# Attention scores in two neighbouring PSUM banks read by one masked maximum, and the outputs moved into the projections' banks

## The chip, the core and the metric

The kernel runs as one program on one core of a Trainium2 chip. A core has a matrix engine (PE, TensorE), whose weight loads are listed apart as PEld, a vector engine (DVE), an activation engine (ACT), GpSimd (POOL) and a queue engine that issues DMAs (SP). Matmul results land in PSUM, which has eight banks of 512 float32 columns on 128 partitions. Each engine works through its own instructions in the order in which the built program lists them, and waits where a semaphore tells it to. The metric is the device time of one execution in microseconds; smaller is better.

## What is computed

The reference is two layers of a diffusion backbone over 512 latent tokens and 256 context tokens of width 1024. The change touches layer 0, a windowed attention with 16 query heads in 4 groups, one key and value head for each group. It is computed in blocks of 128 queries. A latent block sees its neighbours on both sides and all 256 context tokens, and each head has one learned extra logit, the sink:

```python
s_ctx = jnp.einsum('bqkgd,bnkd->bkgqn', qb, k_c) * scale
s_loc = jnp.einsum('bqkgd,bnkd->bkgqn', qb, kb) * scale
s_loc = jnp.where(valid, s_loc, NEG_INF)
p = jax.nn.softmax(jnp.concatenate([s_ctx, s_loc, sink_col], axis=-1), axis=-1)
out = einsum('bkgqn,bnkd->bqkgd', p[ctx], v_c) + einsum('bkgqn,bnkd->bqkgd', p[loc], vb)
```

Context blocks see the 256 context tokens and the sink alone. After the attention come an output projection, a gated feed-forward layer for both streams, and a second layer (a retention mixer and another feed-forward layer).

## The kernel before, in words

The whole program is written with a tile framework: the author writes operations on tiles from pools, and a scheduler fixes the order of the instructions on each engine when the program is built. It takes ready instructions by their place in the source, and a tile of a pool is given out in the order of the source, when the tile that held its buffer before is free. So the pools' buffer counts decide what can run ahead of what.

For each of the 4 groups (line 831) six blocks are attended: four latent blocks of 128 queries (b = 0 to 3) and two context blocks, in an order that differs between the groups (line 833). `attend` (line 760) handles one block:

- `score` (line 678), for each of the 4 heads of the group: matmuls of the head's queries with the keys into a bank (L703), and one DVE instruction (L704) that adds the mask, writes the masked scores to the SBUF tile `pr` and leaves their running extreme in a column of `stat`. Blocks with b = 0 and 3 have 512 keys, context blocks 256: one bank and one instruction. Blocks with b = 1 and 2 have 640 keys, 384 local and 256 of context: two banks and two instructions, the second starting from the first one's result. Every second head, the pair's exponentials (ACT, L101 by its helper), the reciprocal of their sums (DVE, L714) and the scaling (DVE L720 for one head, ACT L718 for the other) follow.
- `turn` (line 724), for each 128 keys: four transposes on PE into a bank of the pool `pT` (L729), and one copy to SBUF (L731, ACT for even pieces, DVE for odd ones).
- `output` (line 736): the products with the values (L743) into a bank `pO`, and a copy out of it (L758, or the two halves of `split` in the last group).

`make_q` (line 559) makes two heads' queries: 24 matmuls of 512 columns for the latent stream and 24 of 256 columns for the context (L147 to L149, by the helper `mm3`), each into a bank `pj`, the square sums that give the norms (L610) into a third `pj` tile, and between them the rotation and the splitting into two parts on DVE and ACT (`shape`, line 581). It is called after the blocks i = 1 and i = 3 of the groups 0 to 2 (line 835), for the next group's heads. In the last group `context_out` (line 818) projects the finished context outputs, each into a `pj` tile.

The eight banks are used thus: two `pj` (projections, line 66), two `pT` (line 283), one `pO` (line 284), three `S2` for scores (line 662). During the set-up before the attention `pO` holds the context keys (`kvc`, line 412), and three banks of a pool that is closed later hold the values (line 413). SBUF buffers that limit how far a block can run ahead: nine `pr` tiles and eight `tt` tiles.

Of the kernel before, what the change touches and what calls it, by code (L numbers as in the profile page):

```python
# [12 lines left out]
ALU = mybir.AluOpType  # L13

P = 128
# [3 lines left out]
SC = 256  # L19
# [30 lines left out]
def dit_kernel(ctx, tc, xT, cT, crow, small, consts, masks, tabs0, tabs1, jtab, adaQ, adaN, adaT, wst, out):  # L50
    nc = tc.nc
    mult, add, sub = ALU.mult, ALU.add, ALU.subtract
# [9 lines left out]
    def T(pool, cols, tag, bufs, dt=F32):  # L62
        return pool.tile([P, cols], dt, tag=tag, bufs=bufs, name=tag)

    def pj(n=512):
        return T(psJ, 512, "pj", 2)[:, :n]
# [33 lines left out]
    def lnexp(*args, **kw):  # L100
        ins = nc.scalar.activation(*args, **kw)  # L101
        after(ins, [turn["pre"]])
        turn["lnexp"].append(ins)
        return ins
# [31 lines left out]
    def next_w(pool, own=2, raw=None, behind=(), late=()):  # L136

        raw = raw or w_raw()
        w = w_parts(pool, own)
        after(split(raw, *w, behind), late)  # L140
        return w
# [21 lines left out]
    def split(t, hi, lo, behind=()):  # L163
        after(nc.scalar.copy(hi, t), behind)  # L164
        return nc.vector.tensor_tensor(lo, t, hi, op=sub)  # L165
# [66 lines left out]
    def h_tiles(s):  # L232
        hi = t_h(s)
        if s == 0:
            return hi, t_h(s)
        return hi[:, 0:SC], hi[:, SC:2 * SC]
# [44 lines left out]
    psA = A.enter_context(tc.tile_pool(name="psA", bufs=1, reuse_waits="tile", space=PSUM))  # L281
    hpool[0] = A.enter_context(tc.tile_pool(name="hA", bufs=1, reuse_waits="tile", side="right"))
    pT = lambda: T(psA, 512, "pT", 2)
    pO = lambda: T(psA, 512, "pO", 1)

    def cond_columns(pool):

# [81 lines left out]
    ps_v = psS.enter_context(tc.tile_pool(name="psS", bufs=1, reuse_waits="tile", space=PSUM))  # L369
# [31 lines left out]
    mask = T(akv, NM * P, "mask", 1, BF16)  # L401
# [7 lines left out]
    wu = [first_unit] + [unit_load(u) for u in UNITS[1:]]  # L409

    kvx = [pj(), pj()]
    kvc = pO()
    kvv = [T(ps_v, 512, "kvv", 3) for _ in range(3)]

    def busy(n):
# [108 lines left out]
    kx, kc = {}, {}  # L524
# [134 lines left out]
        vt.append(v)  # L659
    psS.close()  # L660
    psA2 = At.enter_context(tc.tile_pool(name="psA2", bufs=1, reuse_waits="tile", space=PSUM))
    pS = lambda: T(psA2, 512, "S2", 3)

    run_dep = mybir.DependencyInfo(mybir.DependencyClass.Sync, mybir.DependencyReason.DATA)
    o_raw = {}
# [2 lines left out]
    class Block:  # L668
# [9 lines left out]
        def score(self, i):  # L678
            g, s, b, n = self.g, self.s, self.b, len(self.keys) * P
            hd, nl = 4 * g + i, len(self.lk) * P  # L680
            if i % 2 == 0:
                self.st = T(ap, 16, "stat", 4)
            st, c = self.st, 2 * (b + 4 * s)
            qt = q[hd, s][:, b * P:(b + 1) * P]
            pt = T(ap, 656, "pr", PRB)[:, :n + 1]
            top = stats[hd][:, 1, c + hd % 2:c + hd % 2 + 1]
            nc.gpsimd.tensor_copy(pt[:, n:n + 1], top)
            lo, x0 = st[:, i % 2:i % 2 + 1], self.lk[0] * P if nl else 0

            if nl == 384:  # L690
                runs = [(nl, SC, 5 * P, [(0, SC, kc)]), (0, nl, 2 * P, [(0, nl, kx)])]
            elif nl == 0:
                runs = [(0, SC, 5 * P, [(0, SC, kc)])]
            elif b == 0:
                runs = [(0, n, 3 * P, [(0, nl, kx), (nl, SC, kc)])]
            else:
                runs = [(0, n, 0, [(0, SC, kc), (SC, nl, kx)])]
            for c0, w, m0, parts in runs:
                bank = pS()[:, :w]
                for p0, pw, kk in parts:  # L700
                    for r in range(2):
                        keys = kk[g][r] if kk is kc else kk[g][r][:, x0:x0 + pw]
                        nc.tensor.matmul(bank[:, p0:p0 + pw], qt, keys, start=r == 0, stop=r == 1)  # L703
                nc.vector.tensor_tensor_reduce(pt[:, c0:c0 + w], bank, mask[:, m0:m0 + w], 1.0, top, add, ALU.min, lo)  # L704
                top = lo
            self.pr.append(pt)
            if i % 2 == 0:
                return
            y = stats[hd][:, 0, c:c + 2]
            nc.vector.scalar_tensor_tensor(st[:, 2:4], st[:, 0:2], -1.0, y, mult, mult)  # L710
            for e in range(2):
                pt = self.pr[i - 1 + e]
                lnexp(pt, pt, AF.Exp, scale=y[:, e:e + 1], bias=st[:, 2 + e:3 + e], accum_out=st[:, 4 + e:5 + e])
            nc.vector.reciprocal(st[:, 6:8], st[:, 4:6])  # L714
            for e in range(2):
                pt = self.pr[i - 1 + e]
                if e:
                    nc.scalar.activation(pt[:, :n], pt[:, :n], AF.Identity, scale=st[:, 6 + e:7 + e])  # L718
                else:
                    nc.vector.tensor_scalar(pt[:, :n], pt[:, :n], st[:, 6 + e:7 + e], None, op0=mult)  # L720
            if i == 3:
                self.tt = []
# [12 lines left out]

        def output(self):
            g, s, b = self.g, self.s, self.b
            O = pO()[:, :256]
            for ki, (t, tt) in enumerate(zip(self.keys, self.tt)):
                vg = vt[t][:, g * HD:(g + 1) * HD]  # L740
                f, l = ki == 0, ki == len(self.keys) - 1
                for e in range(2):
                    ins = nc.tensor.matmul(O[64 * e:64 * e + 64, :], vg, tt[:, 256 * e:256 * e + 256], start=f, stop=l)  # L743
                    if f:
                        tc.add_manual_dep(ins.ins, self.last.ins.name, run_dep, reason="value products in one run")
            if g == NKV - 1:
                if b == 0:
                    for e in range(2):
                        o_t[s][2 * g + e] = h_tiles(s)
                for e in range(2):  # L750
                    hi, lo = o_t[s][2 * g + e]
                    cs = slice(b * P, b * P + P)
                    split(O[:, e * P:e * P + P], hi[:, cs], lo[:, cs])
                return
            if b % 2 == 0:
                o_raw[g, s, b // 2] = T(rp, 512, "res", 12)
            dst = o_raw[g, s, b // 2].rearrange("p (e b q) -> p e b q", e=2, b=2)[:, :, b % 2, :]
            nc.vector.tensor_copy(dst, O.rearrange("p (e q) -> p e q", e=2))  # L758

# [102 lines left out]
    for d4 in range(0, KT, 4):  # L862
        wpos[0] = wo0 + max(d4, 2)
        w = [next_w(wo_p) if d > 1 else wo_w[d] for d in range(d4, d4 + 4)]
# [44 lines left out]
    parts = lambda t: (t[:, 0:384], t[:, 384:768])  # L909
    bank = lambda n: T(psF, 512, n, 2)[:, 0:384]  # L910
# [228 lines left out]
    for gsz in FFN_GROUPS:  # L1139
        acts = []  # L1140
        made[:] = 0, gsz
        for i in range(gsz):
            if f < PLAIN:
                acts.append(first[f])
                if f == 1:
                    ends.pop(0)()
            else:
                if f == PLAIN:
                    last_sum()
                a, end = seven()  # L1150
                acts.append(a)
                if f == PLAIN:
                    ends.pop(0)()
                if f == 4:
                    cr = cond_rows(fp)
                if f > 3 and (i or f == 6):
                    ada_next(end)
            if i == 0 and prev is not None:
                output(prev, False)
            f += 1  # L1160
        prev = acts
# [4 lines left out]
    hpool[0] = H.enter_context(tc.tile_pool(name="hR", bufs=1, reuse_waits="tile", side="right"))  # L1166
    wsel[0] = 0
    output(prev, True)
    F.close()
    E.close()  # L1170
# [24 lines left out]
    def chunk(i, own=False):  # L1195
        raw = T(qw, 1024, "wx", 4) if own else T(rp, 1024, "wraw", 2)
        nc.sync.dma_start(raw, wst[i])
        return raw
# [156 lines left out]
    for hd in range(RH):  # L1355
# [24 lines left out]
        Y, X, kc = W4("Y"), W4("X"), W4("X")  # L1380
        kt, qt = [[T(qa, 512, "gate", 4) for _ in range(2)] for _ in range(2)]
# [146 lines left out]
        for i in range(2):  # L1528
            g, v = chunk(bg + i), chunk(bv + i)
# [16 lines left out]
        r, z = mv[:, 8:12], mv[:, 12:16]  # L1546
# [53 lines left out]
        w = []  # L1600
# [188 lines left out]
    for gsz in FFN_GROUPS:  # L1789
        acts = []  # L1790
        for i in range(gsz):
            if f < 2:
                acts.append(first[f])
            elif f == 2:
                w = [next_w(fp, behind=norm_end) for _ in range(2)]
                token_sums(hm, 3, sh2, sA, [weights_end])
                other_parts()
                acts.append(plain(w))
            else:
                acts.append(seven(late))  # L1800
            late = output(prev, False) if i == 0 and prev is not None else ()
            f += 1
        prev = acts
# [146 lines left out]
```

## Time and profile before

| what | before |
|---|---|
| median of 3 runs | 1735.34 us (1734.67 to 1737.06) |
| the profiled execution's own time | 1736.65 us |
| its span, from the first to the last instruction | 1734.9 us |
| PE, DVE, ACT busy over the span | 98%, 79%, 51% |
| granted PE clock, mean over the span | 0.998 |
| HBM read, written | 199.65 MB, 2.10 MB |

The profile is one execution. Its page gives the busy time of each engine, the chain of work that ended last, and groups of equal instructions with their count, busy time, mean duration and what ended the idle time before them. Views of the trace give the same for a stretch of time: what one engine waited for, the chain in order of time, and busy times by windows. A matmul's listed duration includes its way through the array, so successive matmuls overlap and start closer together than their duration. The attention lies between about 98 and 320 us after the span's start. Lines are those of the kernel before; from line 285 on they are one to two lower in the kernel after.

### The profile page before, as it was taken

What the parts mean: (1) busy time and instruction counts of PE and PEld (TensorE: products, weight loads), DVE (VectorE), ACT (ScalarE), POOL (GpSimd) and SP (SyncE); (2) the same over time, 40 slices, a digit from 0 to 9 for tenths busy, and PEclk for the clock granted to TensorE, in tenths of its full rate; (3) what the DMA queues carried; (4) which work ended last, traced back from release to release, by engine and by line L of the source; (5) the groups of instructions that cost most, each with busy time, mean ns of one, the idle gap of its engine ahead of it and who ended that gap; (6) DMA issues with size and microseconds to landing.
All of it is one profiled execution on the core that took longest, in us unless ns stands there. A gap on an engine that the chain in (4) does not pass through costs nothing.

```text
span 1734.9 us, 27679 instructions
## 1 busy us (share of the span) xinstructions
PE 1697.9 (98%) x10876; PEld 1512.6 (87%) x10876; DVE 1368.0 (79%) x2446; ACT 876.4 (51%) x1562; POOL 50.8 (3%) x168
## 2 busy tenths in 40 slices
PE   7999999999999999999999999999999999999999
PEld 5778877899999999999988788898897899899987
DVE  6698888798778788787889858858758798877774
ACT  5588788465433334342455534525525464445442
POOL 0000000000000000000000000000000000000000
PEclk9999999999999999999999999999999999999999
DMA  9601012643254435343423524424433223333322
GB/s 350 237 13 38 13 45 67 209 135 119 73 157 117 152 110 156 122 147 109 147 99 87 182 80 130 162 83 123 157 93 109 88 74 111 109 110 110 98 85 86
DMA packets 59602, 203.54 MB, mean 117 GB/s; under 512 B 6608, under 2 KB 6992, under 8 KB 59216
## 3 DMA queue, kind: packets, MB, share of 16 engines
q1 hardware_dynamic: 51984, 175.03, 31.4%
q0 software_dynamic: 7200, 26.22, 5.2%
q8 instruction: 85, 1.39, 0.3%
q10 hardware_dynamic: 288, 0.52, 0.1%
q14 instruction: 45, 0.37, 0.1%
HBM read 199.65 MB, written 2.10 MB: 116 GB/s over the span
## 4 chain that ended last, share of the span: by engine, by line
PE 71%; DVE 15%; DMA 7%; ACT 4%; issue 2%; SPq 0%; DVEq 0%; ACTq 0%
PE Y L890 13%; PE Z L890 7%; PE pj L147 6%; PE pj L149 6%; PE pj L148 6%; DMA wraw<-in_wst_dram 5%; PE Z L1285 4%; DVE wlo L165 3%; PE X L890 3%; PE pT L729 2%; PE S L703 2%; PE pO L743 2%; PE Y L1274 2%; PE X L1274 1%; ACT whi L164 1%
## 5 line engine op out<-in xcount | busy, mean ns | idle before, releaser
L164 ACT CAST whi<-wraw 128x1024 fp32r<-128x1024 f32 x258 | 270.2, 1051 | 334.6 <-PE Z L149 80.2
L165 DVE TENSOR_TENSOR wlo<-wraw,whi 128x1024 fp32r<-128x1024 f32 x258 | 314.7, 1223 | 64.6 <-ACT whi L164 63.0
L890 PE MATMUL Y<-aq,whi 128*128 128x384 f32 x640 | 173.5, 335 | 0.5 <-ACT hn L1046 0.3
L890 PEld LDWEIGHTS Y<-aq,whi 128*128 128x128 f32 x640 | 116.5, 188 | 1.7 <-ACT hn L1046 1.7
L256 DVE SCALAR_TENSOR_TENSOR res<-pj,mod,res 128x512 f32<-128x512 f32 (+1 forms) x112 | 81.0, 729 | 39.4 <-PE pj L149 39.3
L273 DVE CUSTOM_DVE_ANT_0 y<-adaw,crow,small_sb 128x1024 bf16<-128x1024 f32 x64 | 82.0, 1281 | 34.7 <-DMA adaw<-in_adaT_dram 34.4
L890 PE MATMUL Y<-aq,wlo 128*128 128x384 f32 x320 | 106.9, 334 | 0.0
L1285 PE MATMUL Z<-whi,sA 128*128 128x512 f32 x256 | 81.7, 394 | 1.5 <-ACT gate L1471 1.5
L101 ACT ACTIVATE pr<-pr,stat,qs 128x513 f32<-128x513 f32 (+2 forms) x96 | 74.1, 774 | 14.4 <-DVE stat L710 14.3
L147 PE MATMUL pj<-ax,whi 128*128 128x512 f32 x176 | 69.3, 394 | 2.1 <-DVE res L256 2.1
L149 PE MATMUL pj<-ax,whi 128*128 128x512 f32 x176 | 68.7, 390 | 0.0
L148 PE MATMUL pj<-ax,wlo 128*128 128x512 f32 x176 | 68.6, 390 | 0.0
L147 PE MATMUL pj<-act,whi 128*128 128x512 f32 x168 | 65.6, 390 | 0.0
L148 PE MATMUL pj<-act,wlo 128*128 128x512 f32 x168 | 65.6, 390 | 0.0
L149 PE MATMUL pj<-act,whi 128*128 128x512 f32 x168 | 65.5, 391 | 0.0
L890 PEld LDWEIGHTS Y<-aq,wlo 128*128 128x128 f32 x320 | 60.1, 188 | 0.0
L1285 PEld LDWEIGHTS Z<-whi,sA 128*128 128x128 f32 x256 | 48.0, 188 | 13.1 <-ACT gate L1471 2.7
L890 PE MATMUL Y<-sA,whi 128*128 128x256 f32 x304 | 58.1, 277 | 0.7 <-ACT res L1739 0.7
L729 PE MATMUL pT<-const_sb,pr 128*128 128x128 f32 x352 | 54.3, 281 | 4.2 <-ACT pr L101 1.6
L704 DVE CUSTOM_DVE_ANT_0 pr<-S,mask,qs 128x256 f32<-128x256 f32 (+1 forms) x96 | 53.2, 569 | 6.0 <-PE S L703 4.0
L890 PE MATMUL Y<-hx,whi 128*128 128x256 f32 x304 | 56.2, 277 | 0.0
L729 PEld LDWEIGHTS pT<-const_sb,pr 128*128 128x128 f32 x352 | 39.9, 142 | 14.7 <-issue 4.6
(579 smaller groups left out, 5093.9 us busy)
## 6 DMA issues: line engine op xcount, KB each, us to landing
wraw<-in_wst_dram SPq DMA_DIRECT2D x224, 512.0 KB, 3.7
adaw<-in_adaT_dram POOLq DMA_DIRECT2D x48, 512.0 KB, 3.9
wx<-in_wst_dram SPq DMA_DIRECT2D x30, 512.0 KB, 4.4
adan<-in_adaQ_dram SPq DMA_DIRECT2D x16, 512.0 KB, 7.7
adan<-in_adaN_dram SPq DMA_DIRECT2D x12, 512.0 KB, 7.9
adaw<-in_adaT_dram SPq DMA_DIRECT2D x8, 512.0 KB, 4.2
res<-in_xT_dram SPq DMA_DIRECT2D x14, 256.0 KB, 3.3
aq<-in_adaN_dram SPq DMA_DIRECT2D x12, 256.0 KB, 6.1
```

The lines of the kernel that those rows point to most:

```text
L101: ins = nc.scalar.activation(*args, **kw)
L147: nc.tensor.matmul(o, whi, xhi, start=first, stop=False)
L148: nc.tensor.matmul(o, wlo, xhi, start=False, stop=False)
L149: return nc.tensor.matmul(o, whi, xlo, start=False, stop=last)
L164: after(nc.scalar.copy(hi, t), behind)
L165: return nc.vector.tensor_tensor(lo, t, hi, op=sub)
L256: return nc.vector.scalar_tensor_tensor(res[d], o, mods[l, s][:, part, d:d + 1], res[d], mult, add)
L273: res.append(nc.vector.tensor_tensor_reduce(junk, w, cr[:, s * 1024:(s + 1) * 1024], 1.0, sm_t[:, C_ADAB + l * 48 + j:C_ADAB + l * 48 + j ...
L704: nc.vector.tensor_tensor_reduce(pt[:, c0:c0 + w], bank, mask[:, m0:m0 + w], 1.0, top, add, ALU.min, lo)
L729: nc.tensor.transpose(tp[:, a * P:(a + 1) * P], self.pr[(0, 2, 1, 3)[a]][:, ki * P:(ki + 1) * P], ident)
L890: nc.tensor.matmul(o, p, r, start=first and k + i == 0, stop=k == 3 and i == 2, skip_group_check=not first)
L1285: ins = nc.tensor.matmul(os[t], p, r, start=first and k + i == 0, stop=k == 3 and i == 2, skip_group_check=by_k or not first)
```

## The change

- The pool of scores has two tiles of 1024 columns (two neighbouring banks each) in place of three of 512. A head with 640 keys takes a tile for itself: the 384 local scores in columns 128 to 511, the 256 of context in columns 512 to 767, and one masked maximum reads all 640 columns across the two banks. Two heads with 512 or 256 keys share a tile, one in each bank.
- The local keys come first and the context second in the 640 columns; the mask columns used fit that order.
- The bank `pO` is gone. The outputs of the value products are allocated from the two banks `pj`, together with the projections.
- In the set-up, the context keys' bank is taken from the pool that holds the values.

```diff
-    pO = lambda: T(psA, 512, "pO", 1)
...
-    kvc = pO()
+    kvc = T(ps_v, 512, "kvc", 1)
...
-    pS = lambda: T(psA2, 512, "S2", 3)
+    pS = lambda: T(psA2, 1024, "S2", 2)
...
-            if nl == 384:
-                runs = [(nl, SC, 5 * P, [(0, SC, kc)]), (0, nl, 2 * P, [(0, nl, kx)])]
-            elif nl == 0:
-                runs = [(0, SC, 5 * P, [(0, SC, kc)])]
-            elif b == 0:
-                runs = [(0, n, 3 * P, [(0, nl, kx), (nl, SC, kc)])]
+            if i % 2 == 0 or nl == 384:
+                self.banks = pS()
+            b0 = P if nl == 384 else i % 2 * 512
+            bank = self.banks[:, b0:b0 + n]
+            if nl == 0:
+                m0, parts = 5 * P, [(0, SC, kc)]
+            elif b == 3:
+                m0, parts = 0, [(0, SC, kc), (SC, nl, kx)]
             else:
-                runs = [(0, n, 0, [(0, SC, kc), (SC, nl, kx)])]
-            for c0, w, m0, parts in runs:
-                bank = pS()[:, :w]
-                for p0, pw, kk in parts:
-                    for r in range(2):
-                        keys = kk[g][r] if kk is kc else kk[g][r][:, x0:x0 + pw]
-                        nc.tensor.matmul(bank[:, p0:p0 + pw], qt, keys, start=r == 0, stop=r == 1)
-                nc.vector.tensor_tensor_reduce(pt[:, c0:c0 + w], bank, mask[:, m0:m0 + w], 1.0, top, add, ALU.min, lo)
-                top = lo
+                m0, parts = (3 - (nl == 384)) * P, [(0, nl, kx), (nl, SC, kc)]
+            for p0, pw, kk in parts:
+                for r in range(2):
+                    keys = kk[g][r] if kk is kc else kk[g][r][:, x0:x0 + pw]
+                    nc.tensor.matmul(bank[:, p0:p0 + pw], qt, keys, start=r == 0, stop=r == 1)
+            nc.vector.tensor_tensor_reduce(pt[:, :n], bank, mask[:, m0:m0 + n], 1.0, top, add, ALU.min, lo)
...
         def output(self):
-            O = pO()[:, :256]
+            O = pj(256)
```

## The prediction

> **What bounds the kernel now.** I read the page first, then the stretch of the attention by itself, then who waits for whom there, and last the chain in order of time. From the page:
>
> ```profile
> span 1734.9 us, 27679 instructions
> ...
> PE 1697.9 (98%) x10876; PEld 1512.6 (87%) x10876; DVE 1368.0 (79%) x2446; ACT 876.4 (51%) x1562; POOL 50.8 (3%) x168
> ```
>
> PE is busy for 1697.9 of 1734.9 us, so only a change of PE's gaps or of its work can move the time by much. The change adds and removes no matmul and no transpose. In windows of the trace (columns: stretch, length, busy time of PE, PEld, DVE, ACT, POOL, then granted PE clock, DMA share, GB/s) the attention looks otherwise than the page:
>
> ```profile
> 98.00:320.00 222.00, 212.92 (x1519) 173.84 (x1519) 191.76 (x608) 183.97 (x417) 16.07 (x94) 0.99 0.14 44
> ```
>
> ```profile
> 110.00:120.00 10.00, 9.16 (x71) 7.51 (x70) 9.55 (x35) 8.83 (x19) 1.03 (x4) 1.00 0.00 0
> 120.00:130.00 10.00, 7.40 (x53) 5.15 (x53) 9.63 (x32) 7.75 (x17) 0.62 (x4) 1.00 0.00 0
> ...
> 250.00:260.00 10.00, 6.53 (x41) 4.21 (x42) 9.11 (x33) 8.06 (x20) 0.00 (x0) 1.00 0.04 4
> 260.00:270.00 10.00, 9.43 (x63) 6.89 (x62) 7.54 (x25) 6.82 (x19) 1.26 (x8) 0.83 0.25 80
> ```
>
> Here PE has 212.9 of 222 us, DVE 191.8 and ACT 184.0: three engines near their limits, so the order in which their work interlocks decides. PE's own idle time lies in few places: 120 to 130 (2.6 us) and 250 to 270 (3.5 and 0.6 us, and there the clock is granted at 0.83). DVE is at 9.5 and 9.6 of 10 us from 110 to 130 and at 9.1 from 250 to 260. Who was waited for (us in total, times, longest):
>
> ```profile
> PEld S L703 <- DVE stat L704: 2.9, 8, 0.7
> PE S L703 <- DVE stat L704: 2.8, 4, 1.4
> ```
>
> So PE does wait for the masked maxima, some 5.7 us in all, weight loads included. The chain in order of time (start, length, what, in records; one value product counts as two) shows what else it does:
>
> ```profile
> 126.69 2.38 PE pO L743 x20
> ...
> 141.65 2.31 PE pO L743 x20
> ...
> 178.88 2.31 PE pO L743 x20
> ...
> 231.72 2.38 PE pO L743 x20
> ...
> 313.06 1.88 PE pO L743 x16
> ```
>
> These are the value products of block b = 1 in the groups 0, 1, 2 (126.69, 178.88, 231.72), of b = 2 in group 0 (141.65) and of the last block. A group takes 52.2 and 52.8 us, the rest 81.3.
>
> **The change part by part.**
>
> *One maximum in place of two.* Durations by shape:
>
> ```profile
> L704 DVE CUSTOM_DVE_ANT_0 pr<-S,mask,qs 128x256 f32<-128x256 f32 x64 | 30.0, 480 | 5.8 <-PE S L703 4.0 <-PE pT L729 1.2 <-issue 0.3
> ...
> L704 DVE CUSTOM_DVE_ANT_0 pr<-S,mask,qs 128x512 f32<-128x512 f32 x32 | 23.6, 746 | 0.2
> ...
> L704 DVE CUSTOM_DVE_ANT_0 pr<-S,mask,stat 128x384 f32<-128x384 f32 x32 | 19.5, 611 | 0.8 <-PE S L703 0.2
> ...
> L704 DVE DVE_READ_ACCUMULATOR2_ANT stat<- 128x1 f32 x128 | 10.7, 84 | 0.0
> ```
>
> 32 heads (4 groups, 2 blocks, 4 heads) have 640 keys. From 256 to 384 to 512 columns the mean grows by 131 and 135 ns, so 640 columns are 746 + 135 = 881 ns. A head now pays 480 + 611 + 84 for the second accumulator read; saved are 294 ns, times 32 is 9.4 us of DVE. No row shows a read over two banks. Its bounds are 746 ns (a longer read costs nothing more; saves 13.7 us) and 1175 ns (it costs what two did; saves nothing); I take 881, on the line of the rows. [...]
>
> DVE is not the bound, so only what lies where PE waits for it counts: from 110 to 130 the eight 640-key heads of group 0, 8 x 0.294 = 2.4 us, and two such heads ahead of the first transposes after 250, 0.6 us. I put the gain at **3.0 us**; bounds 0 and 5.7 (all of the waits above).
>
> *Two double banks in place of three single ones.* The built program of after shows the waits. In a 640-key block two heads can be in flight (before, one and a half). In a block with 512 or 256 keys the second head of a pair, though it has a bank of its own, waits in the program for the first head's maximum, since both lie in one tile. So two heads are in flight where three were. The scores of the next blocks are still issued ahead, up to the nine `pr` tiles. I take 0, as the two even out; a loss would be at most the 5.7 us of the waits again.
>
> *Outputs in the projections' banks.* This is the part that decides. Projections (2 tiles and one for the norms for each `make_q`) and outputs now take turns in two banks, in the order of the source. `make_q` after block i = 1 can only begin when that block's output has its bank. In the program of before, the 48 projection matmuls of a `make_q` stand in some 8 to 20 pieces among scores, transposes and outputs; in that of after, all six `make_q` of the loop stand as one unbroken run of 24 + 24, straight after the output of i = 1 or 3. They no longer fill PE's waits in the softmax ahead of them, and while they run, PE feeds neither DVE nor ACT. Rows for the pace of one matmul, and for what follows a run:
>
> ```profile
> 135.19 0.23 PE pj L147
> ```
>
> ```profile
> 245.41 0.79 PE pj L610 x8
> ...
> 246.66 0.87 PE pT L729 x8
> ...
> 249.87 0.52 ACT q L598
> ...
> 250.41 0.68 DVE q L600
> ...
> 251.13 0.69 DVE q L601
> ...
> 251.85 0.42 DVE q L600
> ...
> 252.30 0.42 DVE q L601
> ...
> 256.78 2.75 ACT pr L101 x8
> 259.53 1.01 ACT pr L718 x2
> ...
> 260.56 0.59 ACT tt L731
> ...
> 261.20 2.02 PE pT L729 x9
> ...
> 264.20 2.25 PE pO L743 x16
> ...
> 271.41 0.12 PE pj L149
> ```
>
> ```profile
> L731 ACT COPY tt<-pT 128x512 f32<-128x512 f32 x48 | 27.9, 581 | 9.5 <-PE pT L729 9.0
> L731 DVE COPY tt<-pT 128x512 f32<-128x512 f32 x40 | 27.6, 689 | 7.3 <-PE pT L729 6.8
> ...
> L599 ACT CAST q<-hn 64x512 fp32r<-64x512 f32 x7 | 4.3, 616 | 0.2
> L598 ACT CAST q<-hn 64x512 fp32r<-64x512 f32 x7 | 4.3, 616 | 0.8 <-DVE hn L592 0.8
> ...
> L584 ACT ACTIVATE hn<-pj,qk_gain 128x512 f32<-128x512 f32 x6 | 4.1, 683 | 0.6 <-PE pj L149 0.6
> L585 ACT ACTIVATE sq<-pj 128x512 f32<-128x512 f32 x6 | 3.6, 594 | 0.0
> ```
>
> A run lasts 24 x 0.23 + 24 x 0.12 = 8.4 us. Now the runs one by one.
>
> Runs 1, 3 and 5 (after i = 1). The next block's softmax is done ahead, so PE goes on with transposes. On ACT, the order in after is: L584 and L585 of the latent half (ready at 5.5, done at 6.8), the same of the context half (ready at 8.4; an estimate of 0.8 us, two thirds of the rows' 0.68 + 0.59), two casts of 0.62, two context casts, estimated at 0.4 likewise, and only then the first copy out of `pT`, 0.58: at about 12.0 us from the run's start. On DVE the four low parts (0.68, 0.69, 0.42, 0.42) end at about 12.1 and its first copy at 12.7. PE, after 8.4, has norms and eight transposes (0.79 + 0.34 + 0.87) and six scores (0.7): at 11.1 it stands before a third `pT` tile. Five pieces, two banks, each copy behind the one before: the last copy ends at about 14.7, the ten products take 2.3, so output to output is 17.0 us. In before the same stretch is 143.96 - 129.07 = 14.9. Price **2.1 us** each, 6.3 in all; nearest bounds 1 (the copies find gaps) and 4.
>
> Runs 2, 4 and 6 (after i = 3) make the last heads of the next group. Only two context blocks (run 6: block b = 3 and one of context) are left to fill, and the new group's scores, maxima, exponentials must come one after the other. Before has this once, for group 3, as its projections end at 247: casts and low parts to 252.7, maxima, eight exponentials from 256.78, scaling, and the first long row of transposes at 261.20. Its price stands in the windows from 250 to 270: 3.47 + 0.57 us without PE, and 10 x 0.17 = 1.7 us of clock, 5.7 us. After has it at groups 1 and 2 too: **2 x 5.7 = 11.4 us**; run 6 costs nothing new. The bounds: 2 each (the gap is filled by what is left) and 8.2 (block b = 3 took 266.45 - 252.30 = 14.15 there; 149.91 - 143.96 = 5.95 in group 0, where a row of eight products ends at 148.03 + 1.88).
>
> ```profile
> 148.03 1.88 PE pO L743 x16
> ```
>
> [...]
>
> *Tail.* In group 3, 24 of the context's output projections (24 x 0.12) and five latent ones (5 x 0.23), 4.0 us, stand behind the last value products in after, ahead of them in before. Whether they are missed as filling is open: between 0 and 4.0 us, I take **2.0**. SP issues the same loads, moved by a few places; the windows show its DMAs far from busy. `kvc` in another bank costs nothing: no instruction is added.
>
> Sum: 6.3 + 11.4 + 2.0 - 3.0 = **+16.7 us**. The profiled execution took 1736.65 us (span 1734.9), so 1753.4 for it; the median shown is 1.3 us lower, so the forecast is 1752.0 us. After the attention PE is full until the end, so nothing gives this back.
>
> **The rivals.**
>
> *The maxima were the wait, the runs are free* (other side). Were the next blocks' softmaxes always complete when a run begins, and its casts done in its shade, a run would only move filling and the 9.4 us of DVE would come off wherever DVE leads: 1735.3 - 9.4 = 1726 at best, 1730 with the 5.7 us of waits. It decides if transposes follow each run without a wait. For it: PE waits on L704, nine `pr` tiles. Against it: after runs 2, 4 and 6 the new heads' queries do not exist before the run ends. Chance 0.06.
>
> *Saving and filling cancel.* Runs 2 and 4 cost 2 us each, 1, 3 and 5 1 us, less 5.7: 1736.6. Chance 0.05.
>
> *Every run is a gap.* If PE starves after five of the runs as in group 3's b = 3, with 8.2 us each: +41, 1776. For it: ACT holds casts, exponentials and copies in one queue. Against it: after runs 1, 3, 5 a block is ready. Chance 0.09.
>
> **How the numbers follow.** The forecast's case has 0.80. Its low end is 2 x 2 + 3 x 1 less 3: +4, 1739; its high end 2 x 8.2 + 6 x 2.1 + 4: +33, 1768. The range of 1739 to 1769 leaves out 1726 to 1730, part of the cancelling case and 1776, together under 0.2. About 0.2% (3.5 us) is what a measurement of this kernel can tell from no change. Faster by more 0.06; within it 0.06 (the cancelling case and the forecast's lowest end); slower 0.88.
>
> **What would show it.** In the profile of after: L704 gone in its 384 form, a 640 form near 881 ns, 96 of these instructions in all; six unbroken runs of projections of 8.4 us; PE idle and a lower granted clock 5 to 10 us after runs 2 and 4; groups of about 60 us (52.2 + 2.1 + 5.7) in place of 52; DVE and ACT idle within the runs. Transposes that follow each run at once would make the prediction wrong, as would a 640 form that costs 1175 ns or more, or groups as long as now.

## The result, and the profile after

The changed kernel takes 1774.12 us (median of 5, 1770.05 to 1776.62) against 1734.67 us before (1732.55 to 1737.06): a ratio of 1.0226, 95% interval 1.0215 to 1.0237. It is slower, as forecast, but by 39.5 us and not by 16.7, outside the range. The profiled execution's own time is 1773.39 us. Its page, for the span and the busy times:

```profile
span 1771.6 us, 27582 instructions
...
PE 1710.9 (97%) x10876; PEld 1517.5 (86%) x10876; DVE 1366.2 (77%) x2382; ACT 877.6 (50%) x1562; POOL 50.9 (3%) x168
```

PE is listed 13 us busier with the same number of instructions. The attention by windows, in the columns of the prediction (stretch, length, busy PE, PEld, DVE, ACT, POOL, granted PE clock, DMA share, GB/s), first as one stretch, then in two windows. The first two projection runs begin in the first of them, at 129.6 and 153.3; the second holds the last 1.7 us of the second run and what follows it:

```profile
98.00:355.00 257.00, 223.31 (x1509) 176.84 (x1509) 189.28 (x543) 185.76 (x417) 16.25 (x94) 0.98 0.12 39
```

```profile
130.00:160.00 30.00, 27.84 (x184) 22.62 (x183) 17.25 (x57) 18.63 (x45) 1.16 (x8) 1.00 0.06 19
160.00:190.00 30.00, 24.60 (x172) 19.25 (x170) 25.41 (x68) 22.11 (x47) 2.26 (x16) 1.00 0.06 18
```

The kernel before has, for the same two windows:

```profile
130.00:160.00 30.00, 30.00 (x219) 25.46 (x218) 25.69 (x87) 25.17 (x60) 2.11 (x13) 1.00 0.12 37
160.00:190.00 30.00, 30.00 (x215) 25.26 (x214) 26.80 (x82) 23.50 (x49) 2.05 (x11) 1.00 0.13 36
```

All three engines do in 257 us what took 222; DVE has even 64 instructions less, the 32 second maxima and their accumulator reads. From 130 to 160, where the runs stand, DVE has 17 and ACT 19 of 30 us, in place of 26 and 25; from 160 to 190 PE has 24.6 in place of 30. The engines no longer work at the same time. Who waited for whom in the attention of after:

```profile
ACT hn L583 <- PE pj L149: 34.6, 13, 4.4
...
DVE y L588 <- ACT hn L583: 28.7, 6, 5.4
...
PEld S L702 <- DVE stat L703: 24.6, 39, 2.3
...
PE S L702 <- DVE stat L703: 15.6, 24, 2.1
```

ACT and DVE stand 34.6 and 28.7 us before the results of the projections (3.3 and 1.0 us before). PE stands 15.6 us, its weight loads 24.6, before maxima, in place of 2.8 and 2.9. The new form of the maximum, by shape:

```profile
L703 DVE CUSTOM_DVE_ANT_0 pr<-S,mask,qs 128x640 f32<-128x640 f32 x32 | 27.9, 878 | 3.9 <-PE pT L727 1.7 <-PE S L702 1.3 <-POOL pr L686 0.4
```

878 ns for 640 columns over two banks, where 881 were expected. The chain in order of time, at the outputs of block b = 1 in the groups 0, 1 and 2 (127.30, 190.48, 251.35), of b = 2 in the same groups (144.79, 207.98, 275.34) and at the last output:

```profile
127.30 2.31 PE pj L741 x20
...
144.79 2.38 PE pj L741 x20
...
190.48 2.31 PE pj L741 x20
...
207.98 2.38 PE pj L741 x20
...
251.35 2.38 PE pj L741 x20
...
275.34 2.38 PE pj L741 x20
...
346.08 1.95 PE pj L741 x16
```

To the first of them the two kernels take the same (129.61 and 129.07 at its end). A group, from end to end of these outputs, then takes 192.79 - 129.61 = 63.2 us and 60.9 us, where it was 52.1 and 52.9, and from the third to the last output's end it takes 94.3 where it was 80.8 (348.03 - 253.73; 314.94 - 234.10). What follows the last output takes 1423.6 us, 3.6 more than before. The sum: 0.5 + 11.1 + 8.0 + 13.5 + 3.6 = 36.7 us, the difference of the spans.

Around the first run the chain reads, in the same view:

```profile
129.60 0.43 PE pj L147
...
137.99 0.13 PE pj L149
138.14 0.48 ACT hn L583
...
138.62 0.27 ACT sq L584
138.89 0.61 ACT q L597
139.52 0.62 ACT q L598
140.16 0.41 ACT q L597
140.59 0.40 ACT q L598
141.02 0.27 ACT qs L101
141.29 0.48 ACT tt L729
...
141.82 0.67 PE pT L727 x4
```

The run goes unbroken from 129.60 to 138.1. The latent half's two instructions on ACT have been done within the run; now ACT does the other six that the prediction listed, and a short one for the norms (`qs`, 0.27 us) that it did not list, one after the other. Its first copy out of `pT` ends at 141.8, 12.2 us from the run's start; only then do the transposes of the third piece go on.

### The profile page after: what moved, and what is told of

Read it like the earlier page. It is cut to its first block, busy times and chain, and to the rows that moved or that the text cites. A ratio compares the mean times of both kernels' runs of the same rounds, so it can differ in the third digit from the quotient of the medians.

```text
span 1771.6 us, 27582 instructions
## 1 busy us (share of the span) xinstructions
PE 1710.9 (97%) x10876; PEld 1517.5 (86%) x10876; DVE 1366.2 (77%) x2382; ACT 877.6 (50%) x1562; POOL 50.9 (3%) x168
## 4 chain that ended last, share of the span: by engine, by line
PE 72%; DVE 14%; DMA 6%; ACT 6%; issue 2%; SPq 0%; ACTq 0%; DVEq 0%
PE Y L888 15%; PE Z L888 7%; PE pj L147 7%; PE pj L149 7%; PE pj L148 7%; PE X L888 4%; PE Z L1283 4%; DMA wraw<-in_wst_dram 3%; DVE wlo L165 3%; PE pj L741 2%; DVE pr L703 1%; PE X L1272 1%; PE Y L1272 1%; ACT pr L101 1%; PE pj L1283 1%
## 5 line engine op out<-in xcount | busy, mean ns | idle before, releaser
L703 DVE CUSTOM_DVE_ANT_0 pr<-S,mask,qs 128x512 f32<-128x512 f32 (+2 forms) x96 | 66.6, 700 | 7.0 <-PE pT L727 3.1
```

Of the source, the lines that this page charges most:

```text
L703: nc.vector.tensor_tensor_reduce(pt[:, :n], bank, mask[:, m0:m0 + n], 1.0, top, add, ALU.min, lo)
```

## The experiments

Theory S: the sharing of the two projection banks costs the time, by putting each `make_q` as an unbroken run behind an output. Rival P: the score tiles do, two heads in flight where three were. Medians are against the kernel before in the same series (1734.3 to 1736.2 us), so differences are taken within a series. The ratios are not quotients of these medians; for one pair of kernels the two can disagree by about 1 us.

**e1, the shared banks alone.** On the kernel before:

```diff
-    pO = lambda: T(psA, 512, "pO", 1)
-    kvc = pO()
+    kvc = T(ps_v, 512, "kvc", 1)
-            O = pO()[:, :256]
+            O = pj(256)
```

> The kernel before with one part of the change alone: the outputs of the value products take their tiles from the two projection banks (the output bank is gone, one bank lies unused; scores keep three single banks and two maxima per 640-key head). In the built program each of the six projection runs is again one unbroken run of 48. Theory S (sharing the two banks is the cause): as slow as the changed kernel or a little slower, 1770 to 1785 us, since the saving in maxima is missing. Rival P (the paired score tiles, with two heads in flight where three were, cost most of it): under 1750 us.

Measured: 1769.23 us, ratio 1.0188 (1.0172 to 1.0203), +33.8 us. That is just under the range of theory S and far from that of P: S holds, P falls as the main cause. The six runs are unbroken again. In the 15 us from 98 to 113, where the first `make_q` stood before, PE is now idle for much of the time; first the kernel before, then e1:

```profile
98.00:113.00 15.00, 15.00 (x98) 13.37 (x97) 13.88 (x41) 13.73 (x30) 0.96 (x7) 1.00 0.00 1
```

```profile
98.00:113.00 15.00, 8.42 (x44) 6.31 (x43) 13.61 (x39) 12.39 (x26) 0.95 (x7) 0.81 0.00 0
```

**e8, the order alone.** On the kernel before, with every bank where it was, `make_q` gets the last value product of the block just attended, and its first matmul for each stream is ordered behind it:

```diff
-        nc.tensor.matmul(o, whi, xhi, start=first, stop=False)
+        after(nc.tensor.matmul(o, whi, xhi, start=first, stop=False), behind)
...
-                for piece in make_q(2 * g + 2 + i // 3):
+                for piece in make_q(2 * g + 2 + i // 3, behind=list(ends)):
```

> The kernel before with its banks as they were (outputs in a bank of their own, three single score banks, two maxima), and one order added: the first projection matmul of each call waits, on the matrix engine's own list and without a semaphore, behind the last value product of the block i = 1 or 3. In the built program the six calls are then unbroken runs of 48; the last group's context projections stay spread over 5 to 9 pieces each. Theory S (where the runs stand is the cause, the bank only the means): most of the 34 us of the shared banks, 1758 to 1770 us, the missing part being the last group's. If a bank that is busy too long is the cause: at most 1745 us.

Measured: 1760.25 us, 1.0145 (1.013 to 1.016), +25.9 us. No bank is shared here. The chain of e8, at the outputs of b = 1 in groups 0, 1 and 2 and at the last output:

```profile
126.52 2.38 PE pO L743 x20
...
185.46 2.34 PE pO L743 x20
...
244.20 2.31 PE pO L743 x20
...
338.24 1.88 PE pO L743 x16
```

and that of e1, with its outputs of b = 2 too (144.04, 202.99, 270.43):

```profile
126.47 2.38 PE pj L742 x20
...
144.04 2.38 PE pj L742 x20
...
185.45 2.35 PE pj L742 x20
...
202.99 2.38 PE pj L742 x20
...
244.23 2.31 PE pj L742 x20
...
270.43 2.38 PE pj L742 x20
...
342.48 1.95 PE pj L742 x16
```

Up to the third group the two agree within 0.05 us. So there the loss is all in the order; a wait for a bank adds nothing. They part in the last group, where e8's context projections are still spread.

**e15, the last group's too.** On e8, the first matmul of each `context_out` in the loop is ordered behind its block's output in the same way.

```diff
-                context_out(d, wo_w[d])
+                context_out(d, wo_w[d], list(ends))
```

> The kernel of e8 (the kernel before, its banks as they were, the six projection runs ordered behind the output of their block) with the last group's four context projections ordered behind the outputs of their blocks too, again on the matrix engine's list alone. Their pieces go from 5 to 9 each to one each. Theory S: the rest of what the shared banks cost (e1 at 1769.2 less e8 at 1760.3, 9 us) comes with it, 1766 to 1771 us, of it some 3 us of context matmuls behind the last value product. If the rest is a wait for a bank: it stays at 1762 us or below.

Measured: 1766.71 us, 1.0177 (1.016 to 1.0194), +30.8 us: 4.9 us more than e8 over its own series. It is 3.0 us less than e1's +33.8, with overlapping intervals; what those 3 us are was not settled.

**e3, the projections called ahead of the output.** On the changed kernel:

```diff
+        for piece in between:
+            piece()
         blk.output()
...
-            copy = attend(g, s, b)
-            if not final and i in (1, 3):
-                for piece in make_q(2 * g + 2 + i // 3):
-                    piece()
+            copy = attend(g, s, b, make_q(2 * g + 2 + i // 3) if not final and i in (1, 3) else ())
```

> The changed kernel with the projections called in the source ahead of the output of the block i = 1 or 3, and not behind it; the banks are shared as in the changed kernel. The built program has 4 to 6 pieces per call in place of 2 and the run starts earlier, in the softmax of its block. Theory S in its form 'the place of the run in the order is what costs': a good part comes back, 1745 to 1760 us. If the sharing costs by other waits (an output that waits for the norms' tile), the time stays at 1770 us or above.

Measured: 1769.75 us, 1.019 (1.017 to 1.021), +34.4 us. It lies at the edge of the second expectation, far from the first, so this form of the theory fails: calling them one output earlier gives back some 5 us. The latent half now stands in 3 to 5 pieces, the context half still in one, so the run is almost as solid as it was. So the place by one output is not what counts. That it is the spread over the whole softmax of two blocks fits this, but e3 does not test it by itself.

**e2, outputs in the transposes' banks.** On the changed kernel, one line:

```diff
-            O = pj(256)
+            O = pT()[:, :256]
```

> The changed kernel with one edit: the outputs take their tiles from the two banks of the transposes and not from those of the projections. In the built program the projections stand again in 6 to 17 pieces per call. Theory S: most of the loss is gone, 1725 to 1745 us, and the 9.4 us saved on the vector engine can show. Rival P: the score tiles are unchanged, so it stays above 1755 us. A rival of its own: outputs now hold up the transposes; then 1745 to 1760 us.

Measured: 1738.75 us, 1.0017 (1.0008 to 1.0026), +3.4 us. Both changes to the scores are still in; with the projections spread again, 36 of the 39.5 us are gone. Its window of the attention, and its outputs of b = 1 in groups 0, 1 and 2:

```profile
98.00:320.00 222.00, 213.08 (x1509) 173.61 (x1508) 186.77 (x543) 182.76 (x416) 15.57 (x94) 0.98 0.13 40
```

```profile
127.05 2.38 PE pT L741 x20
...
180.17 2.31 PE pT L741 x20
...
230.64 2.31 PE pT L741 x20
```

PE has 213.1 of 222 us as before the change (212.9), and the groups take 53.1 and 50.5 us.

**e4, two maxima on the double tile.** On the changed kernel:

```diff
-            nc.vector.tensor_tensor_reduce(pt[:, :n], bank, mask[:, m0:m0 + n], 1.0, top, add, ALU.min, lo)
+            for c0, c1 in ((384, n), (0, 384)) if nl == 384 else ((0, n),):
+                nc.vector.tensor_tensor_reduce(pt[:, c0:c1], bank[:, c0:c1], mask[:, m0 + c0:m0 + c1], 1.0, top, add, ALU.min, lo)
+                top = lo
```

> The changed kernel with the 640 columns read by two maxima as before (256 of context, then 384 local), on the same double tile. It prices the merged maximum by itself: 32 instructions and 32 accumulator reads more on the vector engine, 9.5 us of it by the 878 ns that the 640-column form takes. After the runs the vector engine leads, so both theories expect some of it in the time: 3 to 9 us above the changed kernel, 1777 to 1783 us.

Measured: 1778.39 us, 1.0245 (1.0225 to 1.0264), +43.0 us. The merged maximum is worth 43.0 - 39.5 = 3.5 us here, with intervals that overlap. And e4 differs from e1 in the layout of the scores alone: 43.0 - 33.8 = 9.2 us for two double tiles in place of three banks. That is rival P's share: real, and a quarter of the whole. The layout holds a second difference: in e4 PE multiplies the 384 local columns of a head first and the 256 of context second, while the first maximum reads those of context. In e1 context comes first, and its maximum can begin before the local columns are done. No run separates this order from the number of tiles. The waits of PE on maxima grow with the layout; e1's:

```profile
PE S L702 <- DVE stat L703: 7.6, 15, 2.7
```

and e4's:

```profile
PE S L702 <- DVE stat L704: 16.0, 23, 2.1
```

**e16, a double tile for each head.** On the changed kernel, so that no second head waits for the first inside a tile:

```diff
-            if i % 2 == 0 or nl == 384:
-                self.banks = pS()
-            b0 = P if nl == 384 else i % 2 * 512
-            bank = self.banks[:, b0:b0 + n]
+            b0 = P if nl == 384 else 0
+            bank = pS()[:, b0:b0 + n]
```

> The changed kernel with each head of 512 or 256 keys in a double tile of its own; outputs stay in the projection banks and the runs stay unbroken. The paired layout was worth 9.2 us under starvation (e4 at 1778.4 against e1 at 1769.2), and that holds two things: the second head's wait inside a tile, and two heads in flight in place of three. If the wait inside the tile is the price: some 1765 to 1769 us. If it is the number in flight: 1772 to 1776 us, as the changed kernel. Theory S is not touched by either: well above 1755 us.

Measured: 1775.35 us, 1.0231 (1.0214 to 1.0248), +39.2 us, no different from the changed kernel. Here the wait inside the tile is not the price; the number of heads in flight, which is two either way, and the order of a head's two halves are what is left of it.

**e13, e12, e6, e14: the same parts where PE is full.** All have the outputs in the transpose banks. e13 is e1 with `O = pT()[:, :256]` for `O = pj(256)`; e12 is e4 with it; e6 is e16 with it; e14 is e13 with `T(psA2, 512, "S2", 4)`.

> The kernel before with the outputs in the two transpose banks and nothing else (one bank lies unused, three single score banks, two maxima); the projections stand in 9 to 14 pieces per call. It prices the outputs' place by itself and is the base for the next two. Theory S: within 5 us of the kernel before, 1733 to 1741 us. If sharing any two banks costs by waits: 1745 us and above.

> The changed kernel with the outputs in the transpose banks (1738.75 us) and two maxima per 640-key head on the double tile. It prices the merged maximum where the matrix engine is not starved. By the saving under starvation (1778.4 - 1774.1 = 4.3 us) it would be 1743 us; if the matrix engine is full, the vector engine's 9.5 us count for less: 1739 to 1742 us.

> The changed kernel with the outputs in the transpose banks, and each head with 512 or 256 keys in a double tile of its own, so that no second head waits for the first head's maximum in the same tile (still two heads in flight). If that wait is what the paired tiles cost (e4 against e1: 9.2 us under starvation), it comes under the 1738.75 us of the paired form, 1730 to 1736 us. If two heads in flight are the limit either way: 1737 to 1741 us.

> The kernel of e13 (outputs in the transpose banks, three single score banks, two maxima, 1736.0 us against 1734.3) with the free bank given to the scores: four single banks. A candidate for a version faster than both. If the scores' banks limit the matrix engine where it waits for maxima (some 5.7 us in the kernel before): 1728 to 1732 us. If the vector engine's work is the limit there, a bank more is worth nothing: 1734 to 1738 us.

| kernel | scores | maxima per 640-key head | us | ratio (95%) | against before |
|---|---|---|---|---|---|
| e13 | three single banks | two | 1736.00 | 1.0003 (0.9993 to 1.0012) | +1.7 |
| e12 | two double tiles, pairs | two | 1740.61 | 1.0039 (1.0025 to 1.0053) | +6.3 |
| e2 | two double tiles, pairs | one | 1738.75 | 1.0017 (1.0008 to 1.0026) | +3.4 |
| e6 | two double tiles, one head each | one | 1735.98 | 1.0008 (0.9999 to 1.0017) | +1.7 |
| e14 | four single banks | two | 1734.78 | 0.9993 (0.9984 to 1.0002) | -1.1 |

Outputs in the transposes' banks cost nothing that can be measured. The layout with two double tiles costs 4.6 us (e12 less e13; 6 us by the ratios), the merged maximum gives back 2.9 (e2 less e12, intervals that touch), a tile for each head perhaps 1.7 more. e6 came at the upper edge of the range in which the wait inside a tile was to be the price, and e16 in the other one; with intervals that overlap, 1.7 us is not shown. A fourth single bank is worth nothing certain. No version was clearly faster than the kernel before.

## Why the prediction was wrong

**The mechanism and the sign were right, the sum was not.** The part that "decides" did: the shared banks cost 33.8 of 39.5 us (e1), and 25.9 us are lost by the order alone, without any shared bank (e8). Two steps of the prediction failed. It priced the end of the attention, from the output of b = 1 in group 2 on, at 2.1 us for run 5, nothing new for run 6 and 2.0 us for the tail, 4.1 us in all; e1 shows 20.5 us there. And it put the double tiles at 0, by "the two even out"; they cost 9.2 us.

By the ends of the outputs, against the kernel before, in us (one profiled execution of each kernel):

| stretch | forecast for the banks | e1, the banks alone | the changed kernel |
|---|---|---|---|
| to b = 1 of group 0 | 0 | -0.2 | 0.5 |
| to b = 1 of group 1 (runs 1 and 2) | 7.8 | 6.8 | 11.1 |
| to b = 1 of group 2 (runs 3 and 4) | 7.8 | 5.8 | 8.0 |
| to the last output (runs 5 and 6, last group) | 2.1 | 17.1 | 13.5 |
| behind the last output | 2.0 | 3.4 | 3.6 |
| sum | 19.7 | 32.9 | 36.7 |

The terms one by one:

- **Runs 1 and 3, 2.1 us each: nearly right.** Output to output it was 147.17 - 129.61 = 17.6 us, 17.0 forecast, 14.9 before: 2.7 us. In group 1 it was 210.36 - 192.79 = 17.6 us, and 14.4 before: 3.2 us. The list on ACT came in the order written, and ended at 12.2 us for 12.0.
- **Run 5, 2.1 us: wrong.** In group 2 the order of the blocks is another: a context block follows i = 1, and the softmax of b = 2 is ahead only by half: of its four heads' exponentials two start at 252.82 and 253.74, as the run begins, and two at 267.83 and 268.75, after it. From the output of b = 1 to that of b = 2 it took 277.72 - 253.73 = 24.0 us, against 18.2 (252.30 - 234.10): 5.8 us. In e1 it took 272.81 - 246.54 = 26.3 us, 8.1 us more than before. The prediction took "the next block's softmax is done ahead" from group 0.
- **Runs 2 and 4, 5.7 us each: too large for the banks.** In e1 the groups grew by 6.8 and 5.8 us; less the 2.7 and 3.2 that runs 1 and 3 cost there too, this leaves 4.1 and 2.6. In the changed kernel the groups grew by 11.1 and 8.0, which leaves 8.4 and 4.8, but there the double tiles are in it. So it is in part luck that the groups came near the forecast of about 60 us: the double tiles, forecast at nothing, made up for runs that cost less than forecast. The price's part for the clock, 1.7 us, did not come: behind the runs PE has gaps, spread over the stretch, and its clock stays at 1.00, so the price is lost PE time alone. The windows of after in which PE is least busy behind runs 2 and 4:

```profile
170.00:180.00 10.00, 7.80 (x46) 5.87 (x42) 8.48 (x28) 7.32 (x16) 0.79 (x6) 1.00 0.09 36
...
230.00:240.00 10.00, 7.10 (x48) 5.63 (x47) 9.58 (x33) 6.94 (x18) 1.00 (x7) 1.00 0.14 52
```

- **Run 6, nothing new: wrong.** From b = 2 to b = 3 of group 2 it took 16.7 us in after, where the outputs end at 277.72 and 294.44; before it was 14.15. In before those 48 matmuls were in eight pieces, all done before the output of b = 2, so the gap was not yet the whole price. In e1 the same stretch took 18.5 us (272.81 to 291.29). The output of b = 3 in the timeline of PE of after (start, length, what, idle time before it):

```profile
292.49 1.95 PE L741 MATMUL pj<-tt,v 128*64 128x256 f32 x16 [0.18 <-DVE tt L729]
```

- **Tail, 2.0 us: too small.** What stands behind the last output cost 3.6 us, near the 4.0 that was counted, and the last group, without these matmuls between its blocks, grew by 5.1 us more (53.6 for 48.5 from b = 3 of group 2 to the last output; 53.1 in e1). e15 against e8 has 4.9 us for the order of the context projections alone.
- **The maxima, -3.0 us: about right, but mis-placed.** Per head the saving was right (480 + 611 + 84 - 878 ns). The whole merged maximum gave 3.5 us (e4) and 2.9 (e12 to e2), each with intervals that touch or overlap. But the 2.4 us that were to come off before the first output were not seen: that output ended at 129.61 us and at 129.07 before. Nor is it the lost filling that took them, the first `make_q` of the loop, which in the kernel before stands there from 100.7 us on: e1 and e8 lost it too, and their first outputs end at 128.85 and 128.90. PE idles there from 98 to 113, but in the 13 us that follow it is busy for 12.1 us in e1, for 9.9 before. With the double tiles and two maxima, in e4, the output ends at 129.99, and the merged maximum takes 0.4 us off that. These ends lie within 1.14 us of each other, one execution of each kernel; by how much two executions of one kernel differ there is not shown.
- **Two double tiles, 0: wrong.** 9.2 us under starvation (e4 against e1), 4.6 where PE is full (e12 against e13). "The two even out" was argued without a row. PE's waits for maxima went from 7.6 to 16.0 us (e1 to e4). Whether it is the two heads in flight or the order of a head's halves that causes them stays open.

The rival "every run is a gap" came near in size (1776), not in kind: runs 1 and 3 were as cheap as forecast, runs 2 and 4 by themselves cost less, and the rest came from the score tiles and from the end of the attention.

## What to carry to other kernels

A tile pool that gives its buffers out in the order of the source is also an order of the work: two users in one pool cannot pass each other, and matmuls that used to fill the waits of a softmax become a block that the other engines wait for; here the order alone cost 25.9 us (e8). Before moving a tile to another pool, list in the built program where each of the pool's users will stand, and price each group of blocks by itself where the order differs. To tell a wait for a buffer from a place in the order, impose the order on the old kernel without touching its buffers.

## What the hardware showed that was not expected

The granted clock fell in a place where the prediction had no fall, and kept 1.00 behind runs 2 and 4, where it had one. In the changed kernel, while the first scores wait for their maxima, short windows give:

```profile
101.00:104.00 3.00, 0.74 (x4) 0.54 (x4) 2.86 (x10) 2.71 (x6) 0.21 (x1) 1.00 0.00 0
104.00:107.00 3.00, 1.91 (x6) 1.65 (x7) 2.97 (x8) 1.29 (x3) 1.18 (x7) 0.54 0.00 0
107.00:110.00 3.00, 2.15 (x8) 1.56 (x6) 2.91 (x7) 2.88 (x6) 0.00 (x0) 0.50 0.00 0
110.00:113.00 3.00, 1.96 (x8) 1.95 (x8) 2.24 (x8) 2.32 (x5) 0.00 (x0) 0.50 0.00 0
```

The clock is at 0.54 and 0.50 from 104 to 113 us. In the timeline of PE the two longest waits of that time are these (the last columns: idle time before, and what ended it):

```profile
102.26 0.51 PE L702 MATMUL S<-k,q 128*128 128x256 f32 x2 [1.43 <-DVE stat L703]
...
105.09 1.01 PE L702 MATMUL S<-k,q 128*128 128x384 f32 x2 [2.08 <-DVE stat L703]
```

A pair of 384-column score matmuls in the timeline of the kernel before, at a clock of 1.00:

```profile
106.96 0.52 PE L703 MATMUL S<-k,q 128*128 128x384 f32 x2
```

The longest idle time is 2.08 us, and while the clock was halved PE was listed busy for about two thirds of the time, 6.02 of the 9 us from 104 to 113; two matmuls of 384 columns took 1.01 us together in place of 0.52. What these rows show ahead of the fall is a stretch with PE in sparse use, at a clock of 1.00: from 101 to 104 it was busy for 0.74 of 3 us.

The same holds for the fall to 0.83 in the kernel before, from 260 to 270. The longest single idle time ahead of it is 1.56 us:

```profile
259.67 0.96 PE L729 MATMUL pT<-const_sb,pr 128*128 128x128 f32 x6 [1.56 <-ACT pr L101]
```

From 258 to 261 PE was busy for 1.07 of 3 us, at a clock of 1.00; from 261 to 264 the clock was 0.58. On the other side, the two windows behind runs 2 and 4 with PE busy for 7.80 and 7.10 of 10 us kept a clock of 1.00. What in the use of PE lowers the clock was not measured.
